# Turned blocks of the gated features: sixteen transfers inside SBUF, or a write to DRAM and four reads

## The chip, the cores and the metric

The kernel runs on one core of a Trainium2 chip. What counts is the device time of one execution in microseconds (us). A core has TensorE (PE in the profile, its weight loads PEld) for matrix products, VectorE (DVE) and ScalarE (ACT) for element-wise work, GpSimd (POOL, next to idle here), and SyncE (SP), whose queue issues nearly all transfers (DMA). Data live in SBUF, with 128 partitions, in PSUM, where products are summed, and in DRAM. Each engine carries out its instructions in the order in which the program gives them; semaphores make one engine wait for another or for a transfer.

## The reference

One encoder layer on 256 tokens of width 2048, in float32: a mixing part (attention beside a recurrent unit), an FFN, and an input embedding, each with its norms. The change lies in the FFN:

```python
fn = rms_norm(h, g_ffn_pre[i])
ff = (jax.nn.silu(fn @ w_ffn_gate[i]) * (fn @ w_ffn_up[i])) @ w_ffn_down[i]
h = h + rms_norm(ff, g_ffn_post[i])
```

The FFN's inner width is 5632. Before it the kernel forms `fn` without the norm's factor per token; that factor (`rstd_f`) comes in where gate and up are evaluated.

## The kernel before

**Products.** The matrices are float32. Each operand is split into a rounded part `hi` and a remainder `lo`, and a product is three matmuls (hi hi, hi lo, lo hi). The weights come from DRAM in tiles of 512 KB ([128, 2, 512]) on SP's queue (`load_stream`, L436 to L452) into a small ring of raw buffers (`wr`, and some lent ones, `lent_r`). ACT makes `wh` of them (`hi_stream`, L476), DVE subtracts to make `wl` (`lo_stream`, L505), and with that the raw buffer is free for the next load. The split weights stand in another ring of a few buffers until TensorE has used them.

**Groups.** In the FFN, a `Group` computes a 2 x 2 arrangement of blocks: two halves of the tokens (t) by two column blocks of 512; for the gated features, one column block of `w_ffn_gate` and one of `w_ffn_up`. Over the contraction it goes in eight units. A plain unit takes eight block products, a unit of kind "s" seven (Strassen's way), with sums of weights formed on DVE (L525, L529) in buffers `ts` or `lent_t`, and sums of activations held ready. Eight PSUM banks collect a group: `c11`, `c21`, `c12`, `c22`, and `p1`, `p5`, `p6`, `p7`. Consecutive groups swap the two rings of banks.

**What follows a group.** `Seven.early` (L1561) adds up the p banks once the last "s" unit is done: ACT copies p1 into the tile `mid` (L1565), and DVE forms the other three combinations in `mid` and `u_hi`, `u_lo` (L1568 to L1577). `Gated.late` (L1594) adds the c banks (L1647), ACT applies Silu to the gate part (L1654), and DVE multiplies by the up part (L1605). Then `mid` holds 128 tokens per half on the partitions and 512 features along the row. The down projection needs the features on the partitions. This is done in two steps, called the turn here. DVE's transpose turns each 32 x 32 block within its place (L1610). Then blocks must change their partitions: block row a (tokens 32a to 32a+31) of column block c must go to partitions 32c to 32c+31. That is done by sixteen transfers from `mid` to the tile `turned`, SBUF to SBUF, of 32 KB each, on SP's queue (L1639). From `turned`, ACT and DVE make the split operand of the down projection, called `mid0h` and `mid0l` for the first part of the features (L305, L307), and for one block in some groups also the sums that a unit of kind "s" needs (`act_sums`, L1471). The rows of `w_ffn_down` are permuted ahead of time to fit this order of features.

Eleven groups make the gated features, in three parts of four, four and three; after each part follow the groups of the down projection (two, two, and one with two plain column blocks behind it).

**The order of the work.** The order on each queue is written by a planner (`Plan`, L94) while the program is built. It keeps a clock for each engine, gives every step a cost, and lets the tasks, which are generators, take their turn by the time at which they could start plus a "late" value. Where a task yields an `Event`, it goes on when the event's planned time has come. A transfer costs its size over 340 KB per us on the planner's "dma" clock, and what follows it is planned at its end plus LATENCY, 2.0 us (L183). The turn counts as one step of TURN = 4.0 us (L237), so the split of the turned block is planned 6.0 us after the turn can start, and takes its place in the order of ACT and DVE from that. The turn has the late value -4.0. The planned times only set the order; on the chip the waits are real ones.

The tile `turned` lies in the space of `ple0` (L1549); its second half holds activation sums. `mid` has two buffers. DRAM space for things kept aside is in the pool `kept` (L1374).

Of the kernel before, what the change touches and what calls it, by code (L numbers as in the profile page):

```python
# [10 lines left out]
F32 = mybir.dt.float32  # L11
F32R = mybir.dt.float32r
AF = mybir.ActivationFunctionType
ALU = mybir.AluOpType
AX = mybir.AxisListType

P = 128
S = 256
NT = S // P
# [8 lines left out]
N = 512  # L28
# [32 lines left out]
ADDED = 3.0  # L61
LANDED = 6.0
SHARED = 2.6
TURN = 4.0
TURN_LATE = -4.0
DOWN = {
    4: ("p2 p6 s0 p8 p10 s4 p12 p14", "p2 p6 s0 p10 s4 p12 p8 p14"),
# [15 lines left out]
class Event:  # L83


    t = None
# [134 lines left out]
def act(n, tables=COPY, take=None, give=None):  # L221
    return ("act", 0.15 + 0.00082 * n, tables, take, give)


def dve(n, take=None, give=None):
    return ("dve", 0.08 + 0.00104 * n, None, take, give)
# [5 lines left out]

def added(kb):
    return ("sum", kb / 512 * ADDED, None, None, None)


def turn():  # L237
    return ("dma", TURN, None, None, None)


def dma(kb, take=None):
    return ("dma", kb / 340.0, None, take, None)
# [3 lines left out]
def layer(ctx: ExitStack, tc: tile.TileContext, a: dict, out: bass.AP):  # L246
    nc = tc.nc
    const = ctx.enter_context(tc.tile_pool(name="const", bufs=1))
    wp = ctx.enter_context(tc.tile_pool(name="wp", bufs=W_BUFS))
    at = ctx.enter_context(tc.tile_pool(name="at", bufs=1))  # L250
    ps = ctx.enter_context(tc.tile_pool(name="ps", bufs=4, space=bass.MemoryType.PSUM))
    plan = Plan(
        wr=R_BUFS, w=W_BUFS, ts=0, acc=ACC_BUFS, sm=SM_BUFS, ev=1, mid=2, bt=2, uv=1,
    )
# [47 lines left out]
    def split(hi, lo, src, n, give=None):  # L302

        yield act(n)
        nc.scalar.copy(hi, src)  # L305
        yield dve(n, give=give)
        nc.vector.tensor_tensor(out=lo, in0=src, in1=f32(hi), op=ALU.subtract)  # L307
# [32 lines left out]
    def done(event):  # L340
        event.t = plan.now
# [841 lines left out]
    t2 = {}  # L1183
# [138 lines left out]
    def small(n, w=NT):  # L1322
        return const.tile([P, w], F32, name=n)
# [50 lines left out]
    kept = ctx.enter_context(tc.tile_pool(name="kept", bufs=1, space=bass.MemoryType.DRAM))  # L1374
# [85 lines left out]
    def act_sums(x, b, v, form=None):  # L1460

        s = at.tile([P, 4, P], F32, tag="at0_lo", name="s")
        r = [s[:, n, :] if form is None else s[:, n, :].rearrange(form, i=32) for n in range(4)]
        for n, i0, i1, op in (
            (0, v(0, 1), v(1, 1), ALU.add),
            (1, r[0], v(0, 0), ALU.subtract),
            (2, v(0, 0), v(0, 1), ALU.subtract),
            (3, v(1, 0), r[1], ALU.subtract),
        ):
            yield dve(P)  # L1470
            nc.vector.tensor_tensor(out=r[n], in0=i0, in1=i1, op=op)  # L1471
        hi, lo = x.sums[b]
        yield from split(hi, lo, s, 4 * P)
        plan.free["uv"].append(plan.now)
        done(x.ev_sums[b])
# [26 lines left out]
    rstd_f, ev_rf = small("rstd_f"), Event()  # L1502
# [32 lines left out]
    class Mid(Act):  # L1535
# [11 lines left out]
        def open(self):  # L1547
            rs = t2["pool"]
            both = rs.tile([P, 2, 4 * S], F32, tag="ple0", name="turned")  # L1549
            self.raw = both[:, 0, :].rearrange("p (t a n) -> p t a n", a=4, t=NT)  # L1550
            at_ = [both[:, 1, :].bitcast(F32R)]
            if len(self.ev_sums) > 1:
                at_.append(rs.tile([P, 4 * S], F32R, tag="pT", name="sums_m"))
            for k, x in zip(self.ev_sums, at_):
                x = x.rearrange("p (w n m) -> p w n m", w=2, n=4)
                self.sums[k] = x[:, 0, :, :], x[:, 1, :, :]

    class Seven:


        def early(self, g):  # L1561
            bk = g.banks
            yield act(N, take="mid")
            self.e = e = t2["pool"].tile([P, NT, N], F32, tag="mid", name="mid", bufs=2)
            nc.scalar.copy(e[:, 0, :], bk["p1"])  # L1565
            g.give("p1")
            yield dve(N)
            nc.vector.tensor_tensor(out=e[:, 1, :], in0=bk["p6"], in1=e[:, 0, :], op=ALU.add)  # L1568
            g.give("p6")
            yield dve(N, take="uv")  # L1570
            self.u = u = [at.tile([P, N], F32, tag=f"at0_{x}", name=f"u_{x}") for x in ("hi", "lo")]
            nc.vector.tensor_tensor(out=u[0], in0=bk["p5"], in1=e[:, 1, :], op=ALU.add)
            yield dve(N)
            nc.vector.tensor_tensor(out=e[:, 1, :], in0=bk["p7"], in1=e[:, 1, :], op=ALU.add)
            g.give("p7")
            yield dve(N)
            nc.vector.tensor_tensor(out=u[1], in0=bk["p5"], in1=e[:, 1, :], op=ALU.add)  # L1577
            g.give("p5")
            done(g.early)

        def parts(self):
            e, u = self.e, self.u
            return (
                (0, 0, "c11", e[:, 0, :]), (1, 0, "c21", e[:, 1, :]),
                (0, 1, "c12", u[0]), (1, 1, "c22", u[1]),
            )

    class Gated(Seven):

# [4 lines left out]
        def late(self, g):  # L1594
            bk = g.banks
            yield g.early
            e, u = self.e, self.u
            gated = [[Event() for _ in range(2)] for _ in range(NT)]
            for t, c, n, x in self.parts():
                plan.add(self.sum_up(g, n, t, c, x, gated[t][c]), plan.now)  # L1600
            for t in range(NT):
                for ev in gated[t]:
                    yield ev
                yield dve(N)
                nc.vector.scalar_tensor_tensor(  # L1605
                    out=e[:, t, :], in0=u[t], scalar=rstd_f[:, t : t + 1], in1=e[:, t, :],
                    op0=ALU.mult, op1=ALU.mult,
                )
            yield dve(2 * N)
            nc.vector.transpose(e, e)  # L1610
            plan.free["uv"].append(plan.now)
            n = self.kk0 // 4
            if not n:
                self.mid.open()
            raw = self.mid.raw
            there = Event()
            plan.add(self.turn(e, raw, there), plan.now, TURN_LATE)
            yield there
            plan.free["mid"].append(plan.now)
            i, j = divmod(self.kk0, 8)  # L1620
            hi, lo = (x[:, j : j + 4, :].rearrange("p b (c i) -> p c b i", i=32)
                      for x in self.mid.tiles(i))
            raw = raw.rearrange("p t a (b i) -> p (t a) b i", b=4)
            yield from split(hi, lo, raw, 2 * N)
            for b in range(0, 4, 2):
                self.mid.pair(self.kk0 + b)
            for k in self.mid.ev_sums:
                if self.kk0 <= k < self.kk0 + 4:
                    b = k - self.kk0
                    yield dve(1, take="uv")  # L1630
                    yield from act_sums(
                        self.mid, k, lambda j, t: raw[:, 4 * t : 4 * t + 4, b + j, :], "p (a i) -> p a i"
                    )

        def turn(self, e, raw, there):
            yield turn()
            for c in range(4):
                for a_ in range(4):
                    nc.sync.dma_start(  # L1639
                        raw[c * 32 : (c + 1) * 32, :, a_, :],  # L1640
                        e[a_ * 32 : (a_ + 1) * 32, :, c * P : (c + 1) * P],
                    )
            done(there)

        def sum_up(self, g, n, t, c, x, ev):
            yield dve(N)
            nc.vector.tensor_tensor(out=x, in0=g.banks[n], in1=x, op=ALU.add)  # L1647
            g.give(n)
            if c:
                done(ev)  # L1650
                return
            yield ev_rf
            yield act(N, SILU)
            nc.scalar.activation(  # L1654
                self.e[:, t, :], self.e[:, t, :], AF.Silu, scale=rstd_f[:, t : t + 1]
            )
            done(ev)

    class Down(Seven):
# [5 lines left out]
        def late(self, g):  # L1665
            yield g.early
            mg, c0 = t2["mg"], self.c0
            for t, c, n, x in self.parts():
                to = mg[:, t, (c0 + c) * N : (c0 + c + 1) * N]
                if self.part:  # L1670
                    yield dve(N)
                    nc.vector.tensor_tensor(out=to, in0=x, in1=to, op=ALU.add)
                    x = to
                yield dve(N)
                nc.vector.tensor_tensor(out=to, in0=g.banks[n], in1=x, op=ALU.add)
                g.give(n)
            plan.free["mid"].append(plan.now)
            plan.free["uv"].append(plan.now)
            if self.sub:
                for c in range(2):  # L1680
                    yield from self.sub.summed(c0 + c)
# [7 lines left out]
    for part, (f0, f1) in enumerate(parts):  # L1689
        mid = Mid(f"mid{part}", 4 * (f1 - f0))  # L1690
# [206 lines left out]
```

## Time and profile before

| | |
|---|---|
| median of 3 runs | 1207.04 us (1206.78 to 1208.32) |
| the profiled execution's own time | 1205.03 us |
| its span, first to last instruction | 1203.0 us |
| mean granted TensorE clock | 0.988 |
| PE, DVE, ACT busy, share of the span | 96%, 78%, 57% |
| transfers `turned<-mid` | 176, of 32 KB |

A span is the time between the first and the last instruction of the profiled execution. In the views, "L1639" is a line of the kernel, "SPq" the queue of SyncE, `a<-b` an instruction or a transfer that writes a from b. In a timeline the columns are start, duration, engine, line, operation, and in square brackets the idle time of the engine just before and what ended it. A row of the waits says which engine and line waited for which, the total, the number of times and the longest. A row of the stretches gives each engine's busy time and, in brackets, its number of instructions, then the granted clock (PEclk), the busy share of the DMA engines and the rate in GB/s.

### The profile page before, as it was taken

To read this page: it belongs to the slowest core of one execution; us is meant where nothing else is said; L and a number is where in the kernel's file an instruction comes from. 1 tells how busy PE (TensorE), PEld (TensorE's weight loads), DVE (VectorE), ACT (ScalarE), POOL (GpSimd) and SP (SyncE) were. 2 spreads that over 40 slices of the span, in tenths; PEclk is the share of its full clock that TensorE was granted. 3 is DMA by queue.
4 is the path that set the end of the run, shared out by engine and by line. 5 is a ranking of instruction groups with operands and counts; after the bars stand their busy time and mean duration, and the time that the engine had idled before them with its cause. 6 is when DMAs were issued, how large, how long until landed. Compare 5 with 4: busy or idle time off the path is not lost.

```text
span 1203.0 us, 14688 instructions
## 1 busy us (share of the span) xinstructions
PE 1157.9 (96%) x5189; PEld 952.6 (79%) x5189; DVE 941.7 (78%) x1214; ACT 689.4 (57%) x927; POOL 1.6 (0%) x13
## 2 busy tenths in 40 slices
PE   7999999999999999989999999898999998999996
PEld 5888888888888887778788887786888876878885
DVE  6578867877659978987987898797987798788663
ACT  6687787765457663453645446355445355456753
POOL 0000000000000000000000000000000000000000
PEclk9999999999999999999999998999999998999999
DMA  8755556555955775473766556466675465686741
GB/s 311 268 184 181 188 179 187 177 157 181 347 182 179 252 244 182 152 268 141 254 235 192 177 176 206 161 226 200 204 225 181 134 213 181 228 306 218 230 155 70
DMA packets 84425, 244.58 MB, mean 203 GB/s; under 512 B 10368, under 2 KB 27904, under 8 KB 82944
## 3 DMA queue, kind: packets, MB, share of 16 engines
q1 hardware_dynamic: 84208, 243.57, 61.0%
q8 instruction: 40, 0.66, 0.2%
q14 instruction: 33, 0.27, 0.1%
q10 hardware_dynamic: 144, 0.08, 0.0%
HBM read 232.60 MB, written 5.24 MB: 198 GB/s over the span
## 4 chain that ended last, share of the span: by engine, by line
PE 62%; DVE 17%; SPq 8%; DMA 5%; issue 4%; ACT 4%; DVEq 0%; ACTq 0%
PE acc L545 10%; PE acc L544 10%; PE acc L543 10%; SPq L1639 7%; PE c L544 7%; PE c L545 7%; PE c L543 7%; DVE wl L505 6%; ACT wh L476 2%; DMA turned<-mid 1%; PE p L553 1%; PE p L554 1%; PE p L552 1%; DVE lent_t L529 1%; DVE lent_w L505 1%
## 5 line engine op out<-in xcount | busy, mean ns | idle before, releaser
L505 DVE TENSOR_TENSOR wl<-wr,wh 128x1024 fp32r<-128x1024 f32 (+1 forms) x319 | 367.8, 1170 | 78.3 <-ACT wh L476 77.7
L476 ACT CAST wh<-wr 128x1024 fp32r<-128x1024 f32 (+1 forms) x319 | 315.6, 1010 | 139.6 <-PE acc L545 60.0
L544 PE MATMUL c<-wl,hT_mix_hi 128*128 128x512 f32 x436 | 171.5, 393 | 9.4 <-DVE wl L505 9.4
L543 PE MATMUL c<-wh,hT_mix_hi 128*128 128x512 f32 x436 | 171.4, 393 | 1.7 <-DVE mid L1568 1.7
L545 PE MATMUL c<-wh,hT_mix_lo 128*128 128x512 f32 x436 | 171.2, 393 | 0.0
L476 ACT CAST wh<-lent_t 128x1024 fp32r<-128x1024 f32 x65 | 68.1, 1052 | 120.2 <-DVE lent_t L529 93.0
L543 PE MATMUL acc<-wh,hT_hi 128*128 128x512 f32 x320 | 127.9, 400 | 6.7 <-ACT wh L476 6.7
L544 PE MATMUL acc<-wl,hT_hi 128*128 128x512 f32 x320 | 125.6, 392 | 1.9 <-DVE wl L505 1.9
L545 PE MATMUL acc<-wh,hT_lo 128*128 128x512 f32 x320 | 125.4, 392 | 0.0
L544 PEld LDWEIGHTS c<-wl,hT_mix_hi 128*128 128x128 f32 x436 | 82.6, 189 | 27.6 <-DVE wl L505 10.6
L543 PEld LDWEIGHTS c<-wh,hT_mix_hi 128*128 128x128 f32 x436 | 82.4, 189 | 19.4 <-DVE mid L1568 2.4
L545 PEld LDWEIGHTS c<-wh,hT_mix_lo 128*128 128x128 f32 x436 | 82.7, 190 | 17.5 <-DVE hT_mix_lo L313 0.2
L505 DVE TENSOR_TENSOR wl<-lent_t,wh 128x1024 fp32r<-128x1024 f32 x65 | 78.4, 1218 | 12.5 <-ACT wh L476 12.1
L476 ACT CAST wh<-lent_r 128x1024 fp32r<-128x1024 f32 (+1 forms) x61 | 58.7, 979 | 34.8 <-PE c L545 25.1
L505 DVE TENSOR_TENSOR wl<-lent_r,wh 128x1024 fp32r<-128x1024 f32 (+1 forms) x61 | 68.3, 1130 | 10.0 <-ACT wh L476 9.9
L543 PEld LDWEIGHTS acc<-wh,hT_hi 128*128 128x128 f32 x320 | 60.5, 189 | 18.2 <-ACT wh L476 6.7
L544 PEld LDWEIGHTS acc<-wl,hT_hi 128*128 128x128 f32 x320 | 60.4, 189 | 14.9 <-DVE wl L505 3.5
L545 PEld LDWEIGHTS acc<-wh,hT_lo 128*128 128x128 f32 x320 | 60.3, 189 | 12.9
L545 PE MATMUL acc<-wh,hT_ffn_lo 128*128 128x512 f32 x112 | 43.7, 390 | 0.4 <-DVE hT_ffn_lo L313 0.4
L543 PE MATMUL acc<-wh,hT_ffn_hi 128*128 128x512 f32 x112 | 44.0, 393 | 0.0
L544 PE MATMUL acc<-wl,hT_ffn_hi 128*128 128x512 f32 x112 | 43.6, 389 | 0.0
L543 PE MATMUL c<-wh,mid1h 128*128 128x512 f32 x88 | 34.9, 397 | 3.1 <-ACT wh L476 3.1
(440 smaller groups left out, 2233.5 us busy)
## 6 DMA issues: line engine op xcount, KB each, us to landing
wr<-in_w_in SPq DMA_DIRECT2D x79, 512.0 KB, 4.3
wr<-in_w_ffn_down SPq DMA_DIRECT2D x70, 512.0 KB, 4.7
wr<-in_w_ffn_gate SPq DMA_DIRECT2D x64, 512.0 KB, 4.5
wr<-in_w_ffn_up SPq DMA_DIRECT2D x64, 512.0 KB, 4.3
wr<-in_w_out SPq DMA_DIRECT2D x32, 512.0 KB, 4.8
wr<-in_w_ple_gate SPq DMA_DIRECT2D x32, 512.0 KB, 4.6
lent_r<-in_w_ffn_up SPq DMA_DIRECT2D x24, 512.0 KB, 4.2
lent_r<-in_w_ffn_gate SPq DMA_DIRECT2D x24, 512.0 KB, 4.5
```

The source lines that it names most:

```text
L476: nc.scalar.copy(his[i][:, j, :], raws[i][:, j, :])
L505: nc.vector.tensor_tensor(out=los[i][:, j, :], in0=raws[i][:, j, :], in1=f32(his[i][:, j, :]), op=ALU.subtract,)
L529: nc.vector.tensor_tensor(out=t[:, 1, :], in0=first, in1=minus, op=ALU.subtract)
L543: nc.tensor.matmul(accs[t], hi[t], wh[:, j, :], start=st, stop=False)
L544: nc.tensor.matmul(accs[t], hi[t], wl[:, j, :], start=False, stop=False)
L545: nc.tensor.matmul(accs[t], lo[t], wh[:, j, :], start=False, stop=sp)
L552: nc.tensor.matmul(o, lh, wh, start=start, stop=False)
L553: nc.tensor.matmul(o, lh, wl, start=False, stop=False)
L554: nc.tensor.matmul(o, ll, wh, start=False, stop=stop)
L1639: nc.sync.dma_start(raw[c * 32 : (c + 1) * 32, :, a_, :], e[a_ * 32 : (a_ + 1) * 32, :, c * P : (c + 1) * P],)
```

## The change

The tile `mid` is laid out by column blocks, [128, 4, 2, 128] (c, t, n), so that the 1 KB of a partition that belongs to one column block lies in one piece. The evacuations, sums, Silu and gating use views of it in four quarters of 128. After the transpose one transfer writes the whole of `mid` (512 KB) to a DRAM tile `via`, of which there are two. Four transfers read it back, one for each column block c: each writes 32 partitions of `turned`, with the four block rows a side by side (128 KB). The layout of `turned` goes from (t, a, n) to (a, t, n), and the views that read it go with it. The reads depend on the write, so SP waits for its landing ahead of the first of them.

In the plan, the step of TURN goes. The write counts as a transfer of 512 KB (512/340 = 1.5 us); the reads may start its LATENCY and VIA = 1.5 us later, count another 512 KB, and the split is planned their LATENCY and another VIA later. `mid` is given back when the write is planned to have landed, not when the turned data are there. The late value -4.0 stays.

```diff
-TURN = 4.0
+VIA = 1.5
 TURN_LATE = -4.0
...
-def turn():
-    return ("dma", TURN, None, None, None)
...
-            self.raw = both[:, 0, :].rearrange("p (t a n) -> p t a n", a=4, t=NT)
+            self.raw = both[:, 0, :].rearrange("p (a t n) -> p a t n", a=4, t=NT)
...
+    def quarters(x):
+        return x.rearrange("p (c n) -> p c n", n=P)
...
-            bk = g.banks
+            bk = {n: quarters(x) for n, x in g.banks.items()}
             yield act(N, take="mid")
-            self.e = e = t2["pool"].tile([P, NT, N], F32, tag="mid", name="mid", bufs=2)
-            nc.scalar.copy(e[:, 0, :], bk["p1"])
+            self.both = t2["pool"].tile([P, 4, NT, P], F32, tag="mid", name="mid", bufs=2)
+            self.e = e = [self.both[:, :, t, :] for t in range(NT)]
+            nc.scalar.copy(e[0], bk["p1"])
...
             yield dve(2 * N)
-            nc.vector.transpose(e, e)
+            turned = self.both.rearrange("p c t n -> p (c t n)")
+            nc.vector.transpose(turned, turned)
             plan.free["uv"].append(plan.now)
...
-            plan.add(self.turn(e, raw, there), plan.now, TURN_LATE)
+            plan.add(self.turn(raw, there), plan.now, TURN_LATE)
             yield there
-            plan.free["mid"].append(plan.now)
             i, j = divmod(self.kk0, 8)
-            hi, lo = (x[:, j : j + 4, :].rearrange("p b (c i) -> p c b i", i=32)
+            hi, lo = (x[:, j : j + 4, :].rearrange("p b (t a i) -> p t a b i", t=NT, i=32)
                       for x in self.mid.tiles(i))
-            raw = raw.rearrange("p t a (b i) -> p (t a) b i", b=4)
+            raw = raw.rearrange("p a t (b i) -> p t a b i", i=32)
             yield from split(hi, lo, raw, 2 * N)
...
-        def turn(self, e, raw, there):
-            yield turn()
+        def turn(self, raw, there):
+            yield dma(512)
+            via = kept.tile([P, 4, NT * P], F32, tag="via", name="via", bufs=2)
+            nc.sync.dma_start(via, self.both.rearrange("p c t n -> p c (t n)"))
+            out = Event()
+            out.t = plan.now + VIA
+            yield out
+            plan.free["mid"].append(plan.now)
+            yield dma(512)
             for c in range(4):
-                for a_ in range(4):
-                    nc.sync.dma_start(
-                        raw[c * 32 : (c + 1) * 32, :, a_, :],
-                        e[a_ * 32 : (a_ + 1) * 32, :, c * P : (c + 1) * P],
-                    )
-            done(there)
+                nc.sync.dma_start(
+                    raw[c * 32 : (c + 1) * 32].rearrange("j a t n -> j a (t n)"),
+                    via[:, c, :].rearrange("(a j) n -> j a n", a=4),
+                )
+            there.t = plan.now + VIA
```

More of the change, by code (lines that the diff above doesn't have):

```diff
@@ L1556, in open @@
                 self.sums[k] = x[:, 0, :, :], x[:, 1, :, :]
+    def quarters(x):
+        return x.rearrange("p (c n) -> p c n", n=P)
     class Seven:
         def early(self, g):
-            bk = g.banks
+            bk = {n: quarters(x) for n, x in g.banks.items()}
             yield act(N, take="mid")
-            self.e = e = t2["pool"].tile([P, NT, N], F32, tag="mid", name="mid", bufs=2)
-            nc.scalar.copy(e[:, 0, :], bk["p1"])
+            self.both = t2["pool"].tile([P, 4, NT, P], F32, tag="mid", name="mid", bufs=2)
+            self.e = e = [self.both[:, :, t, :] for t in range(NT)]
+            nc.scalar.copy(e[0], bk["p1"])
             g.give("p1")
             yield dve(N)
-            nc.vector.tensor_tensor(out=e[:, 1, :], in0=bk["p6"], in1=e[:, 0, :], op=ALU.add)
+            nc.vector.tensor_tensor(out=e[1], in0=bk["p6"], in1=e[0], op=ALU.add)
             g.give("p6")
             yield dve(N, take="uv")
-            self.u = u = [at.tile([P, N], F32, tag=f"at0_{x}", name=f"u_{x}") for x in ("hi", "lo")]
-            nc.vector.tensor_tensor(out=u[0], in0=bk["p5"], in1=e[:, 1, :], op=ALU.add)
+            self.u = u = [quarters(at.tile([P, N], F32, tag=f"at0_{x}", name=f"u_{x}"))
+                          for x in ("hi", "lo")]
+            nc.vector.tensor_tensor(out=u[0], in0=bk["p5"], in1=e[1], op=ALU.add)
             yield dve(N)
-            nc.vector.tensor_tensor(out=e[:, 1, :], in0=bk["p7"], in1=e[:, 1, :], op=ALU.add)
+            nc.vector.tensor_tensor(out=e[1], in0=bk["p7"], in1=e[1], op=ALU.add)
             g.give("p7")
             yield dve(N)
-            nc.vector.tensor_tensor(out=u[1], in0=bk["p5"], in1=e[:, 1, :], op=ALU.add)
+            nc.vector.tensor_tensor(out=u[1], in0=bk["p5"], in1=e[1], op=ALU.add)
             g.give("p5")
@@ L1582, in parts @@
             e, u = self.e, self.u
-            return (
-                (0, 0, "c11", e[:, 0, :]), (1, 0, "c21", e[:, 1, :]),
-                (0, 1, "c12", u[0]), (1, 1, "c22", u[1]),
-            )
+            return (0, 0, "c11", e[0]), (1, 0, "c21", e[1]), (0, 1, "c12", u[0]), (1, 1, "c22", u[1])
     class Gated(Seven):
@@ L1605, in late @@
                 nc.vector.scalar_tensor_tensor(
-                    out=e[:, t, :], in0=u[t], scalar=rstd_f[:, t : t + 1], in1=e[:, t, :],
-                    op0=ALU.mult, op1=ALU.mult,
+                    out=e[t], in0=u[t], scalar=rstd_f[:, t : t + 1], in1=e[t], op0=ALU.mult, op1=ALU.mult,
                 )
             yield dve(2 * N)
-            nc.vector.transpose(e, e)
+            turned = self.both.rearrange("p c t n -> p (c t n)")
+            nc.vector.transpose(turned, turned)
             plan.free["uv"].append(plan.now)
-            n = self.kk0 // 4
-            if not n:
+            if not self.kk0:
                 self.mid.open()
@@ L1631, in late @@
                     yield from act_sums(
-                        self.mid, k, lambda j, t: raw[:, 4 * t : 4 * t + 4, b + j, :], "p (a i) -> p a i"
+                        self.mid, k, lambda j, t: raw[:, t, :, b + j, :], "p (a i) -> p a i"
                     )
-        def turn(self, e, raw, there):
-            yield turn()
-            for c in range(4):
-                for a_ in range(4):
-                    nc.sync.dma_start(
-                        raw[c * 32 : (c + 1) * 32, :, a_, :],
-                        e[a_ * 32 : (a_ + 1) * 32, :, c * P : (c + 1) * P],
-                    )
-            done(there)
+        def turn(self, raw, there):
[7 more added lines that the diff above has]
+            yield dma(512)
+            for c in range(4):
+                nc.sync.dma_start(
[3 more added lines that the diff above has]
+            there.t = plan.now + VIA
         def sum_up(self, g, n, t, c, x, ev):
             yield dve(N)
-            nc.vector.tensor_tensor(out=x, in0=g.banks[n], in1=x, op=ALU.add)
+            nc.vector.tensor_tensor(out=x, in0=quarters(g.banks[n]), in1=x, op=ALU.add)
             g.give(n)
@@ L1654, in sum_up @@
             nc.scalar.activation(
-                self.e[:, t, :], self.e[:, t, :], AF.Silu, scale=rstd_f[:, t : t + 1]
+                self.e[t], self.e[t], AF.Silu, scale=rstd_f[:, t : t + 1]
             )
@@ L1668, in late @@
             for t, c, n, x in self.parts():
-                to = mg[:, t, (c0 + c) * N : (c0 + c + 1) * N]
+                to = quarters(mg[:, t, (c0 + c) * N : (c0 + c + 1) * N])
                 if self.part:
@@ L1674, in late @@
                 yield dve(N)
-                nc.vector.tensor_tensor(out=to, in0=g.banks[n], in1=x, op=ALU.add)
+                nc.vector.tensor_tensor(out=to, in0=quarters(g.banks[n]), in1=x, op=ALU.add)
                 g.give(n)
```

## The prediction

> **What bounds the kernel now.** I read the busy shares first, then the stretches of the FFN stage, the waits by engine, and one turn in order of time.
>
> ```profile
> span 1203.0 us, 14688 instructions
> PE 1157.9 (96%) x5189; PEld 952.6 (79%) x5189; DVE 941.7 (78%) x1214; ACT 689.4 (57%) x927; POOL 1.6 (0%) x13
> ```
>
> TensorE has work nearly all the time, so what can be won is the time in which it starves. The next view cuts the stage with the eleven turns (400 to 1060 us) into stretches; behind "PE busy" stands in brackets the number of matmuls.
>
> ```profile
> core 0: us, PE busy (x) PEld busy (x) DVE busy (x) ACT busy (x) POOL busy (x), PEclk, DMA share, GB/s
> 400.00:480.00 80.00, 79.16 (x348) 64.69 (x347) 67.39 (x84) 40.22 (x46) 0.00 (x0) 1.00 0.63 208
> 480.00:560.00 80.00, 74.34 (x319) 60.41 (x318) 67.87 (x79) 39.77 (x45) 0.00 (x0) 0.98 0.51 175
> 560.00:640.00 80.00, 78.92 (x347) 64.64 (x346) 68.44 (x78) 41.22 (x44) 0.00 (x0) 1.00 0.71 241
> 640.00:680.00 40.00, 40.00 (x178) 33.13 (x177) 34.90 (x40) 22.44 (x25) 0.00 (x0) 1.00 0.57 183
> 680.00:760.00 80.00, 77.20 (x329) 63.38 (x328) 65.59 (x82) 39.09 (x46) 0.00 (x0) 0.96 0.60 200
> 760.00:840.00 80.00, 72.19 (x302) 58.52 (x301) 66.26 (x76) 39.38 (x44) 0.00 (x0) 0.96 0.58 186
> 840.00:900.00 60.00, 60.00 (x267) 49.67 (x266) 52.12 (x62) 29.48 (x31) 0.00 (x0) 1.00 0.72 226
> 900.00:960.00 60.00, 60.00 (x267) 49.67 (x266) 45.56 (x56) 26.55 (x29) 0.00 (x0) 1.00 0.50 158
> 960.00:1060.00 100.00, 93.18 (x395) 75.40 (x394) 85.55 (x98) 50.75 (x57) 0.00 (x0) 0.97 0.64 213
> ```
>
> Undisturbed, 267 matmuls take 60 us: 0.2247 us each. Each stretch's length less its matmuls at that pace is what it lost: 1.8, 8.3, 2.0, 0, 6.1, 12.1, 0, 0 and 11.2 us, together 41.5 us. What stands behind the loss is in the waits, for ACT, DVE, PE and SP's queue (total us, times, longest):
>
> ```profile
> ACT mid0h L305 <- DMA turned<-mid: 24.8, 4, 7.2
> ACT mid1h L305 <- DMA turned<-mid: 23.0, 4, 6.0
> ACT mid2h L305 <- DMA turned<-mid: 17.7, 3, 6.1
> DVE mid0l L307 <- ACT mid0h L305: 22.4, 4, 6.4
> PE c L544 <- DVE wl L505: 11.1, 5, 4.9
> PE p L553 <- DVE lent_w L505: 6.3, 2, 3.5
> PE p L553 <- DVE wl L505: 1.9, 3, 0.8
> PE c L543 <- DVE mid L1568: 1.7, 1, 1.7
> PE p L552 <- ACT wh L476: 0.6, 2, 0.3
> SPq L451 <- DVE wl L505: 292.1, 154, 9.3
> ```
>
> Every turn makes ACT wait for the turned data: 65.5 us over 11, 5.95 each; DVE waits behind ACT, 22.4 us at the first four. Both are strictly in order, so weight splits queued behind the split of the turned block (L305, L307) are late, and PE ends waiting for wl. The tenth turn in order of time, from SP, ACT, DVE and PE, and then the stretches around it:
>
> ```profile
> 988.57 1.23 DVE L1610 STREAM_TRANSPOSE mid<-mid 128x1024 f32<-128x1024 f32 x1
> 989.83 10.20 SPq L1639 DMA_DIRECT2D turned<-mid  x16
> 1000.14 0.52 SPq L451 DMA_DIRECT2D wr<-in_w_ffn_up  x1
> 1001.42 1.04 ACT L305 CAST mid2h<-turned 128x1024 fp32r<-128x1024 f32 x1 [5.64 <-DMA turned<-mid]
> 1002.50 1.22 DVE L307 TENSOR_TENSOR mid2l<-turned,mid2h 128x1024 fp32r<-128x1024 f32 x1 [5.62 <-ACT mid2h L305]
> 1004.91 0.80 PE L544 MATMUL c<-wl,hT_mix_hi 128*128 128x512 f32 x1 [4.90 <-DVE wl L505]
> ...
> 990.00:999.80 9.80, 9.80 (x45) 7.95 (x43) 6.88 (x9) 2.96 (x3) 0.00 (x0) 1.00 0.18 47
> 1004.90:1010.20 5.30, 5.29 (x13) 4.13 (x13) 5.30 (x7) 4.03 (x5) 0.00 (x0) 0.50 0.86 298
> ```
>
> From the end of the transpose (989.80) to the split (1001.42) 11.6 us pass, 10.2 of them SP issuing sixteen transfers, with the DMA engines 18% busy and every weight load held back. The planner had put the split at TURN 4.0 + LATENCY 2.0 = 6.0 us, so it comes 5.6 us early in ACT's order: ACT's wait of 5.64. Behind the 4.90 us hole the granted clock is 0.50 (13 matmuls in 5.30 us where 23.6 fit), so a long hole costs about half as much again.
>
> **The change part by part.** *Removed and added issues.* These are issues by size and median time to landing, then by issue time (ns) with landing min/median/max, of a gate load, a weight load and today's turn:
>
> ```profile
> kept<-h SPq DMA_DIRECT2D x2, 1024.0 KB, 8.9
> h<-kept SPq DMA_DIRECT2D x2, 1024.0 KB, 6.1
> kept_ple<-ple SPq DMA_DIRECT2D x1, 1024.0 KB, 3.8
> ple<-kept_ple SPq DMA_DIRECT2D x1, 1024.0 KB, 5.7
> ...
> L825 SPq DMA_DIRECT2D av<-in_w_rg_i x8: 378/462/476, 51.8 to 184.2; - x8
> DMA to landing us min/median/max: 2.2/4.3/5.5
> ...
> L451 SPq DMA_DIRECT2D wr<-in_w_ffn_up x64: 327/328/531, 335.3 to 1006.6; - x64
> DMA to landing us min/median/max: 2.8/4.5/8.7
> ...
> L1639 SPq DMA_DIRECT2D turned<-mid x176: 587/595/1346, 413.2 to 1044.9; - x176
> ```
>
> SP's stretch of 10.2 us goes. In its place come one write of 512 KB in rows of 4 KB, a wait on SP until it has landed, and four reads of 128 KB in rows of 1 KB. The write: no store of this size is in the trace; it lies between 2.8 us (fastest 512 KB weight load) and 8.9 (the 1 MB store kept<-h under load); I take 4.5, the median of the weight loads, which have its size and rows. Four issues: 0.33 to 0.60 us each; I take 0.46 (the gate load av, 128 KB in several runs). Landing of the last read: 2.2 to 5.5; I take 4.3, the median of the same row, for its equal size. Round trip: 4.5 + 3 x 0.46 + 4.3 = 10.2 us; bounds 2.8 + 1.0 + 2.2 = 6.0 and 8.9 + 1.8 + 5.5 = 16.2.
>
> The Trainium skill ("DMA: Bandwidth & Descriptors", section "Anatomy of one DMA — SWDGE (gpsimd) path") speaks against the change: a semaphore fires only after the receipt of the last byte, and of the wait it says "This can cause a surprisingly long delay especially when the write target is HBM"; here two such receipts stand in series where there was one. Its fit, made for the other path, of 2.0 us plus size over 436 GB/s gives as an estimate 3.2 us for the write and 2.3 for a read, and a round trip near 7 us. The trace goes both ways: stored and read back, h took 8.9 and 6.1 us, ple 3.8 and 5.7.
>
> *Moved due time.* The plan now counts 512/340 = 1.5, latency 2.0 and VIA 1.5 for the write, and the same for the reads: the split is due 10.0 us behind the transpose, not 6.0. This is the larger half: the data take 10.2 us instead of 11.6, hardly faster, but ACT and DVE get 4 us more of weight splits ahead of it. The lateness falls from 5.95 to 0.2.
>
> *What is queued between and behind.* Loads that the plan places in the 5.0 us between write and reads (two or three by its 1.5 us each) go out meanwhile, where they wait today. A load that waits for its buffer holds up the reads: SP waits 292.1 us over 154 times, 1.9 us a time, mostly at moments other than this one. I add 0.8 us (0 to 1.9). The wait for the landing holds loads back too, 4.5 us at most less what went out between; today it is 10.2. So the split is about 1 us late at each turn.
>
> *Layout.* mid goes from (t, n) to (c, t, n): copies, sums, gating and Silu then go in runs of 128 elements, the split in runs of 32 as today. Cost nil: the split with runs of 32 takes 1.22 us (row above), a contiguous weight split of the same size has the same 1.22:
>
> ```profile
> 1003.64 1.22 DVE L505 TENSOR_TENSOR wl<-lent_r,wh 128x1024 fp32r<-128x1024 f32 x1
> ```
>
> To the last digit shown, 0.01 us, the nine operations of a group would cost 0.1 us, 1 us over eleven. mid comes free at the landing of the write, about when it did. The added 0.5 MB each way go into DMA engines at 0.50 to 0.72 of their time; the 18% of the row above show the room.
>
> *Sum.* 41.5 us of loss per 65.5 us of ACT's waiting is 0.63 us of TensorE time per us of lateness. Three rows of PE's waits I do not put down to the turns, as short ones at splits of sums or at banks not yet cleared: 1.9 + 1.7 + 0.6 = 4.2. One us of lateness costs 11 x 0.63 = 6.9. Gain 41.5 - 4.2 - 6.9 = 30.4. The profiled execution took 1205.03 us itself (span 1203.0, 2.0 around it), which gives 1174.6; the median of the runs, 1207.04, stands 2.0 above it: **1177 us**. With the bounds of the round trip: at 6.0 us no lateness, 37.3 us gain, 1170; at 16.2 + 0.8, 7.0 us late, 48.5 + 4.2 - 41.5 = 11.2 us lost, 1218.
>
> **The rivals.**
>
> *DVE is the next bound.* Per matmul DVE worked 67.87/319 = 0.213 us in 480 to 560 and 85.55/395 = 0.217 in 960 to 1060: 95 to 96% of TensorE's 0.2247, so it can hardly catch up, and the bursts at a group's end (four sums, two gatings, transpose, split) stay. Against it: 840 to 900 runs at full pace with DVE at 52.12 of 60. If the bursts keep half of today's loss, 20.8 + 4.2 us stay, the gain is 16.5: 1190.
>
> *All of it goes, and more.* With loads no longer held 10 us, the remaining PE waits go too: 37 to 42 us, 1165 to 1170. For it: the first turn (issues from 413.2, row above) lies in the stretch that lost 1.8 us, so a small lateness may be swallowed by the buffers of split weights; against: the tight DVE.
>
> *The reads get stuck (slower).* SP is one queue. If a load placed between write and reads waits for a buffer that DVE gives back late (longest 9.3 us), the reads wait with it, and DVE in turn waits for them. It decides from a round trip of 10.0 + 5.95 = 16 us on; at 17.5 us on average the time is (7.5 - 5.95) x 11 x 0.63 = 10.7 us above today: 1218. Against it: the plan orders the loads by when buffers come free.
>
> *It doesn't do what it says.* The round trip takes some 16 us and the later due time is just used up: no change, 1207.
>
> **How the numbers follow.** Forecast (1170 to 1184) 0.5, DVE bound (1184 to 1203) 0.21, everything (below 1170) 0.16, reads stuck 0.09, used up 0.04. Faster by over 0.2% (about 2.4 us, what a measurement of this kernel can tell) 0.87, within it 0.04, slower 0.09. The range of 1164 to 1198 leaves out some 0.04 below and 0.16 above.
>
> **What will show it.** Right, if ACT's waits for turned fall from 65.5 us to 5 to 20, the landing of the write is 3.5 to 6 us and that of the reads 2.5 to 5, SP's turn has five issues with loads between write and reads, and the stretches of 80 us hold 345 or more matmuls with PEclk at 1.00. The due time as the larger half is wrong if the data now come in 8 us or less. The forecast is wrong if SP waits long between write and reads, or PE still waits for wl while ACT no longer waits for turned.

## The result and the profile after

The changed kernel takes 1166.63 us (median; 1206.91 for the kernel before, timed beside it): 0.9658 of the time before, 95% interval 0.9639 to 0.9677. One of its four executions took 2361.22 us, for a reason that nothing here shows; the median counts it, the ratio does not. Timed again later (e9 below) it took 1165.86 us, 0.9665 (0.9651 to 0.9678). The forecast was 1177, so the gain of 40 us is ten more than forecast; it is what the rival "all of it goes, and more" gave.

The lines of the changed kernel have other numbers: the write is L1634, the reads L1641, the split of the turned block L301 (ACT) and L303 (DVE), the weight splits L472 and L501, sums of weights L521 and L525, the transpose L1608. The head of its page, and the stretches of the FFN stage:

```profile
span 1162.7 us, 14552 instructions
PE 1144.1 (98%) x5189; PEld 948.0 (82%) x5189; DVE 942.7 (81%) x1214; ACT 692.2 (60%) x927; POOL 1.6 (0%) x13
...
480.00:560.00 80.00, 80.00 (x355) 66.26 (x354) 76.44 (x88) 45.86 (x52) 0.00 (x0) 1.00 0.75 248
760.00:840.00 80.00, 80.00 (x354) 66.26 (x354) 76.30 (x89) 43.21 (x49) 0.00 (x0) 1.00 0.70 227
960.00:1040.00 80.00, 80.00 (x355) 66.26 (x354) 72.08 (x83) 45.32 (x55) 0.00 (x0) 1.00 0.81 270
```

TensorE is never idle here, at the full clock, with 354 or 355 matmuls in 80 us where it had 302 and 319. To see where the 40 us went, the whole stage of both kernels; first before, then after, each with the 400 us ahead of it:

```profile
0.00:400.00 400.00, 389.93 (x1855) 323.58 (x1856) 292.44 (x437) 277.78 (x433) 1.60 (x13) 1.00 0.64 213
400.00:1080.00 680.00, 655.01 (x2825) 536.08 (x2824) 569.94 (x669) 341.83 (x380) 0.00 (x0) 0.98 0.62 204
```

```profile
0.00:400.00 400.00, 391.45 (x1856) 325.20 (x1857) 292.66 (x437) 278.25 (x433) 1.59 (x13) 1.00 0.64 214
400.00:1040.00 640.00, 640.00 (x2826) 530.10 (x2825) 573.97 (x673) 344.62 (x381) 0.00 (x0) 1.00 0.70 226
```

Up to 400 us hardly anything changed. The same 2825 matmuls (2826 by the second row) then took 680 us before and take 640 now; 40.0 of the 40.3 us by which the span is shorter come from this stage. The waits that answer to those of before (total us, times, longest), the whole of PE's own list among them, and issue times (ns) with landing (us, min/median/max) of the write and the reads:

```profile
ACT mid0h L301 <- DMA turned<-via: 9.2, 3, 4.1
ACT mid1h L301 <- DMA turned<-via: 4.5, 3, 2.4
ACT mid2h L301 <- DMA turned<-via: 2.1, 2, 1.4
SPq L1641 <- DMA via<-mid: 9.9, 8, 2.3
PE acc L539 <- ACT wh L472: 6.7, 1, 6.7
PE pg L326 <- DVE xcl L303: 0.9, 3, 0.5
PE acc L540 <- DVE wl L501: 0.8, 1, 0.8
PE acc L541 <- DVE hT_ffn_lo L309: 0.4, 1, 0.4
...
L1634 SPq DMA_DIRECT2D via<-mid x11: 326/326/327, 412.8 to 996.3; - x11
DMA to landing us min/median/max: 2.6/2.9/5.1
...
L1641 SPq DMA_DIRECT2D turned<-via x44: 319/422/437, 416.1 to 1002.1; - x44
DMA to landing us min/median/max: 2.6/4.9/7.7
```

ACT's waits for the turned data fell from 65.5 to 15.8 us; of PE's waits none lies in the stage (the 6.7 us is the kernel's start). The tenth turn again, in the timelines of DVE, SP and ACT:

```profile
952.27 1.25 DVE L1608 STREAM_TRANSPOSE mid<-mid 128x1024 f32<-128x1024 f32 x1
953.54 0.33 SPq L1634 DMA_DIRECT2D via<-mid  x1
954.68 0.33 SPq L447 DMA_DIRECT2D wr<-in_w_ffn_gate  x1
957.02 0.33 SPq L447 DMA_DIRECT2D wr<-in_w_ffn_up  x1
957.44 1.80 SPq L1641 DMA_DIRECT2D turned<-via  x4
959.35 0.37 SPq L447 DMA_DIRECT2D wr<-in_w_ffn_gate  x1
964.98 1.05 ACT L301 CAST mid2h<-turned 128x1024 fp32r<-128x1024 f32 x1 [1.37 <-DMA turned<-via]
```

From the end of the transpose (953.52) to the split 11.5 us pass, where it was 11.6. The turn is no faster here; over the eleven turns it is 10.6 us on average (9.0 to 12.6), against 11.8. But two loads go out while the write lands and a third right behind the reads, where SP was taken for 10.2 us, and ACT waits 1.37 us in place of 5.64.

### The profile page after: what moved, and what is told of

Its sections match the earlier page's. It is cut to its first block, busy times and chain, and to the rows that moved or that the text cites. A ratio compares the mean times of both kernels' runs of the same rounds, so it can differ in the third digit from the quotient of the medians.

```text
span 1162.7 us, 14552 instructions
## 1 busy us (share of the span) xinstructions
PE 1144.1 (98%) x5189; PEld 948.0 (82%) x5189; DVE 942.7 (81%) x1214; ACT 692.2 (60%) x927; POOL 1.6 (0%) x13
## 4 chain that ended last, share of the span: by engine, by line
PE 92%; DVE 3%; ACT 2%; DMA 2%; SPq 1%; issue 1%; DVEq 0%; ACTq 0%
PE c L539 14%; PE c L541 14%; PE c L540 14%; PE acc L541 11%; PE acc L540 11%; PE acc L539 11%; PE p L548 3%; PE p L550 3%; PE p L549 3%; PE c L548 2%; PE c L549 2%; PE c L550 2%; DMA av<-in_w_rg_i 1%; DVE wl L501 1%; PE tr L321 1%; ACT wh L472 1%
## 5 line engine op out<-in xcount | busy, mean ns | idle before, releaser
L501 DVE TENSOR_TENSOR wl<-wr,wh 128x1024 fp32r<-128x1024 f32 (+1 forms) x319 | 368.1, 1170 | 87.7 <-ACT wh L472 87.1
L472 ACT CAST wh<-wr 128x1024 fp32r<-128x1024 f32 (+1 forms) x319 | 317.3, 1012 | 164.8 <-PE acc L541 70.5
L472 ACT CAST wh<-lent_t 128x1024 fp32r<-128x1024 f32 x65 | 68.0, 1053 | 117.8 <-DVE lent_t L525 84.4
L501 DVE TENSOR_TENSOR wl<-lent_t,wh 128x1024 fp32r<-128x1024 f32 x65 | 78.1, 1219 | 13.5 <-ACT wh L472 13.2
L472 ACT CAST wh<-lent_r 128x1024 fp32r<-128x1024 f32 (+1 forms) x61 | 58.8, 981 | 32.5 <-PE c L541 25.6
L501 DVE TENSOR_TENSOR wl<-lent_r,wh 128x1024 fp32r<-128x1024 f32 (+1 forms) x61 | 68.3, 1129 | 8.3 <-ACT wh L472 8.2
```

What stands on the lines that cost most here:

```text
L472: nc.scalar.copy(his[i][:, j, :], raws[i][:, j, :])
L501: nc.vector.tensor_tensor(out=los[i][:, j, :], in0=raws[i][:, j, :], in1=f32(his[i][:, j, :]), op=ALU.subtract,)
```

## The experiments

The change does two things at once: the split of the turned block is planned later (10.0 us behind the transpose, not 6.0), and SP's queue is free for loads during the turn. Four runs take them apart. Theory D is the prediction's: the due time is the larger half. Theory Q: the loads held back by SP's sixteen issues (the hold, from here on) are what starves TensorE.

**e1, the later due time alone.** In the kernel before:

```diff
-            done(there)
+            there.t = plan.now + 4.0
```

> The kernel before, its sixteen transfers inside SBUF kept, with one thing changed in the plan: the split of the turned block is planned 10.0 us behind the transpose, as in the changed kernel, not 6.0. Theory D (the due time is the larger half): the data still take 11.6 us, so the split comes 1.6 us early in place of 5.6; ACT's waits for turned fall from 65.5 to about 18 us, and at 0.63 us of TensorE time per us of lateness 11 us of loss stay beside the 4.2 that are not the turns': 1207 - 41.5 + 11 + 4 = 1181 us (1172 to 1187). Theory Q (SP's 10.2 us of issues, which hold the weight loads back, are what starves TensorE): the time stays at 1197 us or more, with ACT or DVE waiting for wr in place of turned.

Measured 1193.27 us, ratio 0.9884 (0.9869 to 0.9899): between the two, a third of the gain.

**e2, due at 12.0 us.**

```diff
-            done(there)
+            there.t = plan.now + 6.0
```

> As e1, with the split planned 12.0 us behind the transpose, later than the data come (11.6 us). Theory D: no lateness is left, ACT's waits for turned under 8 us, 1207 - 41.5 + 4 = 1170 us (1165 to 1175): as fast as the changed kernel, without any trip through DRAM. Theory Q: 1195 us or more, as e1.

Measured 1199.43 us, 0.9931 (0.9912 to 0.9951). Theory D falls: no lateness to speak of is left, and four fifths of the loss are still there. Its waits, and its third turn in the timelines of SP and DVE, show what took the place of ACT's wait:

```profile
ACT mid0h L305 <- DMA turned<-mid: 6.4, 3, 3.6
ACT mid1h L305 <- DMA turned<-mid: 3.5, 2, 1.9
ACT mid2h L305 <- DMA turned<-mid: 1.3, 1, 1.3
DVE lent_t L525 <- DMA wr<-in_w_ffn_up: 30.7, 10, 6.3
DVE lent_t L525 <- DMA wr<-in_w_ffn_down: 15.2, 3, 7.5
DVE lent_t L525 <- DMA lent_r<-in_w_ffn_up: 12.2, 5, 6.2
ACT wh L476 <- DMA wr<-in_w_ffn_down: 26.9, 7, 8.5
PE c L543 <- ACT mid2h L305: 5.9, 1, 5.9
...
506.27 10.19 SPq L1639 DMA_DIRECT2D turned<-mid  x16
516.57 0.52 SPq L451 DMA_DIRECT2D wr<-in_w_ffn_gate  x1
517.19 0.38 SPq L451 DMA_DIRECT2D wr<-in_w_ffn_up  x1
521.97 0.69 DVE L525 TENSOR_TENSOR lent_t<-wr 128x512 f32<-128x512 f32 x1 [4.20 <-DMA wr<-in_w_ffn_up]
```

ACT's 65.5 us became 11.2, and DVE's waits for raw weights went from 9.2 to 58.5. DVE now gets as far as a sum of weights whose load stood behind the sixteen issues, and stands still there for 4.20 us. Its half of the split of the turned block, whose data ACT had taken up at 517.92, stands behind that sum. ACT stands still for held loads too: its waits for raw weights between 390 and 1070 us are 39.6 us, 17.0 before. At the eleventh turn it waits 8.21 us for a load of `w_ffn_down` that SP issued behind the sixteen, its split of the turned block stands behind that, and TensorE waits 5.9 us for the split.

**e3, the plan told how long SP's queue is taken.** One number in the kernel before:

```diff
-TURN = 4.0
+TURN = 9.5
```

> The kernel before with TURN = 9.5 in place of 4.0 alone: the plan now counts SP's queue as taken for 9.5 us, about what its sixteen issues take (10.2), and so also plans the weight loads behind the turn as late as they really come; the split is due at 9.5 + 2.0 = 11.5 us. Theory D: as e2, 1165 to 1175 us, the order of the loads changing nothing. Theory Q: better than e1 and e2 by 5 us or more, since weight splits are planned around the held loads, but over 1185 us.

Measured 1165.29 us, 0.9651 (0.9637 to 0.9666): the whole gain of the change, with the sixteen transfers and their 10.2 us left as they are. The stage of e3:

```profile
400.00:1040.00 640.00, 640.00 (x2825) 529.85 (x2824) 574.13 (x672) 345.15 (x381) 0.00 (x0) 1.00 0.64 217
...
956.59 10.19 SPq L1639 DMA_DIRECT2D turned<-mid  x16
```

So the held queue costs nothing once the plan counts it. What costs is an order of ACT's and DVE's work that does not reckon with it. Theory Q's 1185 or more falls too.

**e4, the new path with the old due time.** In the changed kernel:

```diff
-            there.t = plan.now + VIA
+            there.t = plan.now + VIA - 4.0
```

> The changed kernel, with its write and four reads, but the split planned 6.0 us behind the transpose as in the kernel before (the planned time of the turned data is taken 4.0 us earlier; write and reads stand where they did). Theory D: the data take 9.0 to 10.5 us, so the split is 3 to 4.5 us early, 33 to 50 us of waits on ACT, and 0.63 of that is lost: 1188 to 1198 us. Theory Q: the loads go out between write and reads, so the loss is small whatever the due time: 1175 us or less.

Measured 1181.92 us, 0.9802 (0.9773 to 0.9831), with 45.5 us of ACT's waits for turned: between the theories again. With the loads flowing, 29.7 us more of these waits than in the changed kernel (15.8) cost 15 us, about 0.5 us per us.

On these I formed theory H: the hold is the main thing, the lateness the smaller. The next four runs test it.

**e5, the hold planned, the lateness not.** TURN = 9.5 as in e3, but the split due at 6.0 us:

```diff
-            done(there)
+            there.t = plan.now - 5.5
```

> The kernel before with the plan's step on the transfer clock at 9.5 us, as in e3, but the split due at 6.0 us, as before: the held loads are planned, the lateness of the turned data (5.6 us a turn) is not. Theory H (formed on e1 to e4: what costs most is that DVE and ACT are given work in an order that counts on weights which SP's queue holds back; the lateness of the split is the smaller part): a loss like that of e4, 12 to 16 us behind e3's 1165: 1177 to 1182 us. Theory D (the due time is the larger half): 1188 to 1198 us, 30 us or more of ACT's waits for turned turning into 20 us or more of loss.

Measured 1205.74 us, 0.9988 (0.9973 to 1.0003). Both theories fall: nothing clear of the noise is gained. Its waits for turned are those of before (25.8 + 23.4 + 17.5 = 66.7 us), and so are DVE's behind ACT's half of the split (61.6 us, 61.7 before); those of DVE for raw weights are small (7.4 us):

```profile
ACT mid0h L305 <- DMA turned<-mid: 25.8, 4, 7.2
ACT mid1h L305 <- DMA turned<-mid: 23.4, 4, 6.5
ACT mid2h L305 <- DMA turned<-mid: 17.5, 3, 6.0
DVE mid0l L307 <- ACT mid0h L305: 22.6, 4, 6.6
DVE lent_t L525 <- DMA lent_r<-in_w_ffn_up: 4.1, 3, 2.4
```

**e6, sixteen reads in place of four**, the plan and all else as in the changed kernel:

```diff
             for c in range(4):
-                nc.sync.dma_start(
-                    raw[c * 32 : (c + 1) * 32].rearrange("j a t n -> j a (t n)"),
-                    via[:, c, :].rearrange("(a j) n -> j a n", a=4),
-                )
+                for a_ in range(4):
+                    nc.sync.dma_start(
+                        raw[c * 32 : (c + 1) * 32, a_, :, :].rearrange("j t n -> j (t n)"),
+                        via[a_ * 32 : (a_ + 1) * 32, c, :],
+                    )
```

> The changed kernel with sixteen reads of 32 KB in place of four of 128 KB and the same plan, so that all else stands in the same order: SP's queue is taken for 7 to 9.5 us (16 x 0.42 to 0.60) after the write has landed, some 10 us without loads in a plan that counts 1.5, and the turned data come after 13 to 15 us in place of 10. Theory H: the held loads and a lateness of 3 to 5 us bring back a loss like e1's or more, 1190 to 1207 us. Theory that the trip through DRAM by itself (one write, SP free while it lands) is what freed TensorE: 1175 us or less.

Measured 1181.25 us, 0.9794 (0.9777 to 0.9811), better than theory H allowed and worse than the other: 47.4 us of ACT's waits, 6.9 of DVE's for raw weights. Four reads rather than sixteen are worth 15 us under the plan of the change.

**e7, e2 with the sixteen transfers on GpSimd's queue:**

```diff
-                    nc.sync.dma_start(
+                    nc.gpsimd.dma_start(
...
-            done(there)
+            there.t = plan.now + 6.0
```

> e2 (sixteen transfers inside SBUF, split due at 12.0 us) with the sixteen issued on GpSimd's queue, idle here, in place of SP's; the order of all else is that of e2. Theory H: with SP's queue free the loads go on as planned, and e2's loss of 34 us goes but for what the data come later than 12 us: 1165 to 1175 us if they come within 13 us, and 0.3 to 0.6 us per us and turn more beyond. Theory D: e2's loss stays, 1195 us or more.

Measured 1175.15 us, 0.9746 (0.9722 to 0.9771). With SP's queue free, 24 of e2's 1199.43 us go and DVE's waits for raw weights fall from 58.5 to 8.6 us. But the data come later from this queue: a transfer lands 4.3 us behind its issue at the median, where it was 1.9 in e2, the split starts 14.8 us behind the transpose on average, and ACT waits 42.5 us. The time is what theory H gave for data that late. Taken with e2 this is the run that shows the hold as a cause, by taking it away and leaving the order.

**e8, sixteen transfers inside SBUF in the new layout**, with e3's plan:

```diff
-            yield dma(512)
-            via = kept.tile([P, 4, NT * P], F32, tag="via", name="via", bufs=2)
-            nc.sync.dma_start(via, self.both.rearrange("p c t n -> p c (t n)"))
...
+            yield ("dma", 9.5, None, None, None)
             for c in range(4):
-                nc.sync.dma_start(
-                    raw[c * 32 : (c + 1) * 32].rearrange("j a t n -> j a (t n)"),
-                    via[:, c, :].rearrange("(a j) n -> j a n", a=4),
-                )
-            there.t = plan.now + VIA
+                for a_ in range(4):
+                    nc.sync.dma_start(
+                        raw[c * 32 : (c + 1) * 32, a_, :, :].rearrange("j t n -> j (t n)"),
+                        self.both[a_ * 32 : (a_ + 1) * 32, c, :, :].rearrange("j t n -> j (t n)"),
+                    )
+            done(there)
```

> The layouts of the changed kernel (1 KB in one piece per partition and column block), but sixteen transfers inside SBUF and the plan of e3 (step of 9.5 us, due at 11.5): no trip through DRAM. If an issue takes its time by the number of pieces (32 in place of 64), it falls from 0.6 to 0.33 to 0.45 us; if not, it stays. Theory H: the plan then counts the hold as long as it is or longer, so in both cases 1163 to 1168 us.

Measured 1165.54 us, 0.9663 (0.9648 to 0.9677), as theory H had it. The layout neither costs nor brings anything, and issues of 32 pieces take as long as those of 64.

The eight runs gave theory J: the early split and the unplanned hold fill the same ten us of a turn. Whichever is taken away, DVE and ACT stand still in them for the other; TensorE loses nothing once both are gone, by either path. The last four runs test that, and the price of a us of lateness.

**e9 and e10, the changed kernel and e3 side by side**, no edits beyond theirs.

> The changed kernel again, for a comparison side by side with e10. Theory J (formed on e1 to e8: the early split and the unplanned hold of the loads fill the same ten us of a turn, so that either alone keeps most of the loss, and TensorE loses nothing once both are gone, by whichever path): 1164 to 1168 us.

> e3 again (sixteen transfers inside SBUF, TURN = 9.5), beside e9. Theory J: 1164 to 1168 us, within 3 us of e9. If the trip through DRAM is worth something of its own, e10 is slower than e9 by 3 us or more.

Measured 1165.86 us, 0.9665 (0.9651 to 0.9678), and 1164.96 us, 0.9655 (0.9641 to 0.9668). The intervals overlap: the trip through DRAM shows no worth of its own beside a plan that counts the sixteen issues.

**e11, e6 with the plan told of it:**

```diff
-            yield dma(512)
+            yield ("dma", 7.0, None, None, None)
...
-            there.t = plan.now + VIA
+            done(there)
```

> e6 (write to DRAM, sixteen reads), whose turned data come 13 to 15 us behind the transpose, the slowest turn of all, with the plan told so: the reads count 7.0 us on the transfer clock in place of 1.5, and the split is due at 14.0 us. Theory J: 1163 to 1169 us, though the turn takes longer than before the change. If the speed of the turn matters: as e6, 1178 us or more.

Measured 1166.78 us, 0.9674 (0.9659 to 0.9689). Its turns take 11.9 to 15.4 us, 14.1 on average, longer than the 11.8 before the change, and nothing is lost. How fast the turn is does not matter within these bounds; that the plan knows its length does.

**e12, the changed kernel with the split due at 8.0 us:**

```diff
-            there.t = plan.now + VIA
+            there.t = plan.now + VIA - 2.0
```

> The changed kernel with the split due at 8.0 us, between e4 (6.0) and itself (10.0); ACT's waits for turned near 28 us, between 45.5 and 15.8. My price of the prediction, 0.63 us of TensorE time per us of lateness: about 7 us of loss more than the changed kernel, 1173 to 1176 us. A cover, in which the first three or four us of waiting at a turn cost nothing and those behind it more than 0.63 each: 1168 us or less.

Measured 1168.78 us, 0.9688 (0.9673 to 0.9703), with 27.7 us of ACT's waits: 2 to 3 us over the changed kernel, nearer the cover than the straight price.

The runs side by side, ordered by the sum of the two waits (ACT for the turned data, DVE for raw weights to be summed; both over the whole run, in us):

| kernel | turn, split due | ACT for turned | DVE for raw | sum | time |
|---|---|---|---|---|---|
| e11 | DRAM, 16 reads, planned; 14.0 | 11.5 | 4.5 | 16.0 | 1166.8 |
| e8 | SBUF, new layout, hold planned; 11.5 | 14.0 | 6.1 | 20.1 | 1165.5 |
| e3 | SBUF, hold planned; 11.5 | 14.9 | 6.4 | 21.3 | 1165.3 |
| changed (e9) | DRAM, 4 reads; 10.0 | 15.8 | 5.6 | 21.4 | 1165.9 |
| e10 | as e3 | 15.6 | 6.1 | 21.7 | 1165.0 |
| e12 | DRAM, 4 reads; 8.0 | 27.7 | 12.4 | 40.1 | 1168.8 |
| e7 | GpSimd's queue; 12.0 | 42.5 | 8.6 | 51.1 | 1175.2 |
| e6 | DRAM, 16 reads, unplanned; 10.0 | 47.4 | 6.9 | 54.3 | 1181.3 |
| e4 | DRAM, 4 reads; 6.0 | 45.5 | 13.2 | 58.7 | 1181.9 |
| e2 | SBUF, unplanned; 12.0 | 11.2 | 58.5 | 69.7 | 1199.4 |
| e1 | SBUF, unplanned; 10.0 | 27.1 | 43.5 | 70.6 | 1193.3 |
| e5 | SBUF, hold planned; 6.0 | 66.7 | 7.4 | 74.1 | 1205.7 |
| before | SBUF, unplanned; 6.0 | 65.5 | 9.2 | 74.7 | 1206.9 |

Up to a sum of 40 us, or 3.6 a turn, the times lie within 4 us. From 51 to 75 they rise by 32, some 1.3 us per us. The sum orders the runs only roughly: e1 is 6 us faster than e2 at nearly the same sum, and it leaves out ACT's waits for raw weights, 35 and 40 us in e1 and e2 (390 to 1070 us), 10 to 25 in the others. That the first us at each turn are covered by weights already split, and that the halved clock behind a long hole makes the rest cost more than itself, fits the rows of the prediction (the 4.90 us hole, the clock of 0.50); the cover was not measured by changing the number of buffers.

## Why the prediction was right, and where it was not

*What bounds the kernel.* The reading held. The stage was put at 41.5 us of loss; 40 were won, and no idle time of TensorE is left there. The floor of the sum, 1205.03 - 41.5 = 1163.5, was nearly reached.

*The sum.* Two terms were too large, and they make up the ten us between 1177 and 1166.6. The three rows of PE's waits that I did not put down to the turns (4.2 us) are gone too, in e3 as well. That they were after-effects of the turns is likely and not shown: they lay 20 to 35 us behind a transpose. And the price of lateness (6.9 us for one us a turn) was taken as a straight line through zero, 0.63 us per us. The lateness came out as forecast, 15.8 us of ACT's waits against a forecast of 11, but no idle time of TensorE is left from it. In e12 27.7 us of these waits, 2.5 a turn, cost 2 to 3 us more than the changed kernel's 15.8, where the line gives 7: it has a flat start. The first turn, which waited and lost little, stood among the rival's reasons and was the better guide.

*The round trip.* 10.2 us and 0.8 for loads between; measured 10.6 on average. This closeness is in part luck, as two errors inside it cancel: the write landed in 2.9 us, not 4.5 (nor in the 3.5 to 6 named as a sign), and the reads in 4.9 at the median of all four, not 4.3, the last of a turn in 4.5 to 7.8 where ACT waited for it. Of the Trainium skill's two statements ("DMA: Bandwidth & Descriptors", section "Anatomy of one DMA — SWDGE (gpsimd) path"), the fit, made for the other path, gave an estimate of 3.2 us for the write, near the 2.9 measured; the long delay of a receipt from HBM does not show here, and the reads took twice the fit's estimate of 2.3 us. One or two loads went out between write and reads at ten of eleven turns, as the plan has it; SP waited for the landing 9.9 us over eight times. The reads never got stuck (they went out 2.6 to 5.2 us behind the write), so the slower rival fell.

*The due time as the larger half.* This step was wrong as the prediction put it. The due time alone brought 14 us (e1) or 8 (e2), and the old due time on the new path still gained 25 (e4). But the opposite is wrong as well: planning for the hold alone brought 1 us, which the noise covers (e5). The halves do not add up, since both hold DVE and ACT up in the same ten us. That the total came out within ten us all the same is luck in this step: the sum charged the whole loss to the lateness, and the change ends lateness and hold together. Of e2, which ends the lateness alone, the same price made 1170, and it took 1199. The sign set for this step, data within 8 us, did not come (the split began 9.0 us behind the transpose at the earliest), so it could not show the error. What I had not put into the sum is that the later due time sends DVE on to sums of weights whose loads SP holds back; I had named that cover ("4 us more of weight splits ahead of it") without asking whether their weights would be there.

*DVE as the next bound* fell: in 480 to 560 us DVE is now busy 76.44 of 80 us, and TensorE still never waits.

## What to carry to other kernels

Where the order of the work is written by a plan, the first thing to hold against the trace is what the plan believes of each step: here one number, 4.0 us for a step that takes SP's queue for 10.2, cost 42 us (e3), and changing it alone won as much as the new path. Two waits that lie in the same stretch hide each other; taking one away then shows little, and only runs with both, each and neither tell what they are worth together. A price per us of waiting taken from a run that is deep in waits is too high for small ones.

## What the runs showed of the hardware

In these runs SP's time for one issue went by the kind of transfer, not by its number of pieces. The first row is of the kernel before (SBUF to SBUF, 64 pieces of 512 B), then e8 (the same, 32 pieces of 1 KB), e6 (DRAM to SBUF, 32 pieces of 1 KB), with min/median/max in ns:

```profile
L1639 SPq DMA_DIRECT2D turned<-mid x176: 587/595/1346, 413.2 to 1044.9; - x176
```

```profile
L1635 SPq DMA_DIRECT2D turned<-mid x176: 512/589/1656, 414.5 to 1006.1; - x176
```

```profile
L1642 SPq DMA_DIRECT2D turned<-via x176: 302/419/1681, 416.2 to 1022.6; - x176
```

The four reads of the changed kernel, with four times the pieces of e6's, take 422 ns each, and its write 326. And a store of 512 KB landed sooner (2.9 us at the median) than a weight load of that size (4.5); the two did not run beside the same traffic, so this is no comparison of the directions by themselves.
